# A depthwise convolution's running sums in a PSUM tile of two banks, and two banks instead of four for small products

## The chip, the cores and the metric

The kernel runs on one core of a Trainium2 chip. The core has five engines with instruction streams of their own: TensorE (PE; its weight loads are listed as PEld), VectorE (DVE), ScalarE (ACT), GpSimd (POOL) and SyncE (SP), which issues nearly all DMAs here. The metric is the device time of one execution in microseconds; lower is better.

## What is computed

The reference is one inference step of a decoder with two layers, for a prompt of 512 tokens (with 16 leading tokens before it) and eight samples of 8 tokens. The change touches layer 0. There one input projection feeds two branches: A, a gated unit, a causal depthwise convolution of width 31, a LayerNorm over channels, a swish and a projection; and B, a complex state space (S5) with its own projections. Each branch is gated, and an output projection follows:

```python
def _conformer_conv(u, g, buf, conv_w, conv_b, ln_g, ln_b, pw):
    h = u * jax.nn.sigmoid(g)
    hp = jnp.concatenate([buf.astype(h.dtype), h], axis=1)
    y = lax.conv_general_dilated(hp, conv_w.astype(h.dtype)[:, None, :], window_strides=(1,), padding='VALID',
                                 dimension_numbers=('NWC', 'WIO', 'NWC'), feature_group_count=W_A)
    y = y + conv_b.astype(h.dtype)
    y = jax.nn.silu(_ln(y, ln_g, ln_b)).astype(u.dtype)
    y = y @ pw.astype(u.dtype)
    return y, hp[:, -(CONV_W - 1):]

def _even_layer(x, conv_buf, s_re, s_im, ev, j):
    proj = x @ ev['w_in'][j].astype(x.dtype)
    u_a, g_a, z_a, u_b, z_b = _split(proj, EVEN_SIZES)
    y_a, new_buf = _conformer_conv(u_a, g_a, conv_buf, ...)
    y_b, new_re, new_im = _s5(u_b, s_re, s_im, ...)
    mix = jnp.concatenate([y_a * jax.nn.silu(z_a), y_b * jax.nn.silu(z_b)], axis=-1).astype(x.dtype)
    out = mix @ ev['w_out'][j].astype(x.dtype)
    ...
```

Layer 1 (an mLSTM branch and an RWKV branch) is not touched.

## The kernel before, in words

All 592 token columns (528 of the prompt with its leading tokens, 64 of the samples) stay on chip with channels on the 128 partitions. A projection goes by stripes of 128 output columns: for each of the 16 blocks of inputs, the weights are split into a high part `wh` (a cast on ACT) and a low part `wl` (a subtraction on DVE, from `wraw` and `wh`), the operands likewise into `xh` and `xl`, and PE adds three products for each of two spans of 296 columns into two PSUM banks of the tag `acc`. The weights come in pieces of four blocks, with two buffers each of `wh` and `wl`; one piece feeds 24 products.

Layer 0's first part runs as a set of threads in `layer0` (line 843). `Weave.run` (line 323) chooses at build time the order of each engine's instructions, by an estimated timeline with costs per instruction (`cost`, line 239) and a priority for each thread; on the chip every engine takes its stream in that order. A thread can ask for a PSUM bank by its tag and wait for it. Beside the four `acc` banks, four banks have the tag `sps`, for small products: the S5 tables (`s5_inject_tables`, `s5_tables`), the S5 injections and outputs (`s5_inject`, `s5_out`), the LayerNorm's sums (`ColNorm`) and, at the start, the third stripe of the first bundle of projections. ACT copies the small products out (`s5m`, `s5xv`, `s5kt`, `s5y`).

The threads around the change: `convs` (line 1033) calls `conv_taps` (line 831) for each of eight channel blocks. The input `hh` of a block is made on DVE from a projection's PSUM banks and a gate (`glu`, line 912). The block's result `cc` is made by 31 taps, each of two DVE instructions, one over the 528 prompt columns and one over the 64 sample columns: the first tap a tensor_scalar, the other 30 a scalar_tensor_tensor that multiplies a shifted view of `hh` by the tap's weight (a column of `par`) and adds `cc`, into `cc`. `norms` then subtracts the shift from `cc` on POOL, squares it on ACT and adds both to the sums on POOL. `s5_chain` is a recurrence over 66 chunks for each half of the states, with three small POOL products a step (tiles `s5c` and `s5xv`). After the norms and S5's outputs, `norms` makes the operands `cbh` and `cbl` of the next projection. The gate stripes of the input projection (`gates`) are spread between the convolution's blocks by the number of finished blocks, `S.taps`; those that are left follow.

All instructions that go through the threads are recorded under one line, L321, so that the tiles' names tell them apart.

Of the kernel before, what the change touches and what calls it, by code (L numbers as in the profile page):

```python
# [11 lines left out]
F32 = mybir.dt.float32  # L12
F32R = mybir.dt.float32r
# [7 lines left out]
NT = 592  # L21
K1, K2 = 354, 532            # columns of parameters and constants of RWKV, where layer 0 has two of S5's tables
NP = 528
SPAN0 = ((0, 296), (296, 592))
SPAN1 = ((16, 304), (304, 592))
SPANR = ((14, 302), (302, 592))            # the leading tokens have no outputs; the last one shifts into the prompt
SPAN2 = ((16, 336), (336, 592))
NZ = 5           # gate stripes with the RWKV phase
MIX1 = [8, 9, 10, 11, 12, 13, 0, 1, 2, 3, 4, 5, 14, 15, 6, 7]     # as they become ready
# [7 lines left out]
# ------------------------------------------------------------------ host side  # L37

def _consts():
    """Shape-only constants, packed: of both layers, of RWKV, of mLSTM."""  # L40
# [16 lines left out]
    # mLSTM: invalid entries carry 200  # L57
# [10 lines left out]
    c["rreset"] = np.broadcast_to(reset, (128, 128))       # of a chunk, of the samples  # L68
    c["own"] = (p[:, None] // 16 == np.arange(64)[None, :] // 8) & (p[:, None] % 8 == np.arange(64)[None, :] % 8)
    # rows of a sample token: K = high, low, high part; V = high, high, low part  # L70
# [19 lines left out]
def _gp(v):  # L90
    """[64 groups, 64 states, ...] -> [(g2, p), g', ...]"""
    v = v.reshape((32, 2, 64) + v.shape[2:])
    v = np.moveaxis(v, 0, 2)
    return v.reshape((128, 32) + v.shape[3:])
# [14 lines left out]
def layout(x):  # L109
# [48 lines left out]
        x["state_mlstm_c"][0].reshape(8, 4, 2, 128, 256).transpose(1, 0, 3, 2, 4))   # h b kp kb v  # L158
    a["rs0"] = np.ascontiguousarray(
        x["state_rwkv_s"][0].transpose(1, 3, 0, 2).reshape(8, 128, 8, 64))            # pair (h k) b v  # L160
# [6 lines left out]
    a["w_m"] = _stripes(np.concatenate([w[:, 0:4096], w[:, 4104:5128]], 1))           # q k v o zc  # L167
# [3 lines left out]
    a["w_r"] = _stripes(w[:, 5128:9352])                                              # r k v wa zd  # L171
# [16 lines left out]
def unlayout(r):  # L188
# [3 lines left out]
    conv = r["o_conv"].transpose(1, 2, 0)                                     # 9 30 1024  # L192
# [10 lines left out]
# ---------------------------------------------------------------- device side  # L203
# [5 lines left out]
class Engine:  # L209
    """An engine whose instructions are emitted later: each call gives one to yield."""  # L210
# [11 lines left out]
def delay(p, e):  # L222
    """us from a result of engine p to its use by engine e."""
    if p == e:
        return {"G": 0.1, "D": 2.0}.get(e, 0.0)
    if e == "T":
        return {"A": 0.3, "V": 0.23, "G": 0.2}.get(p, 1.2) + MT
    return {"T": 0.2, "G": 0.08, "D": 1.2}.get(p, 0.14) + (MV if e == "V" else MA)


def part(z):
    """What of a tile an operand is."""
    return z.name, z.offset, tuple(z.ap)


SAME = {"V": 0.13, "A": 0.14}              # us from a result to its use by the same engine


def cost(e, fn, out, ins):
    """Estimate in us."""  # L240
# [6 lines left out]
    cols = sum(z.shape[1:] == (1,) for z in ins) * (n > 1)         # per-partition scalars  # L247
# [15 lines left out]
class Weave:  # L263
    """Emits threads of instructions, with each engine's in the order of an estimated timeline.  A thread yields
    instructions, conditions to wait for, or the tag of a PSUM bank to get.  Low priority numbers go first."""
# [13 lines left out]
    def ready(self, op):  # L279
        """When an instruction's operands are there."""  # L280
# [3 lines left out]
        for z in ins + [out]:  # L284
            f, p = self.done.get(z.name, (0.0, e))
            if z is not out or e != "D" or p != "D":          # loads of parts of a tile don't wait for each other
                t = max(t, f + delay(p, e))
            if p == e and e in SAME:
                t = max(t, self.at.get(part(z), 0.0) + SAME[e])
# [33 lines left out]
    def run(self, threads):  # L323
        """threads: (priority, generator)."""
# [44 lines left out]
def both(*gens):  # L369
    """Emits generators by turns; their values."""  # L370
# [11 lines left out]
def run(gen):  # L382
    """Emits a generator straight; its value."""
# [7 lines left out]
def straight(K, gen):  # L391
    """Emits a thread without a Weave; its value."""
# [48 lines left out]
def resident(K, pool, W, s):  # L441
    """Stripe s of W, split, all of it on chip."""
# [11 lines left out]
def dense_s(K, ws, rhs, span, out=None):  # L454
    """Products of several resident stripes over one span, by turns."""
# [11 lines left out]
def weights(K, W, s, k0):  # L467
    """Blocks k0 .. k0 + 4 of W's stripe s as exact parts."""
# [11 lines left out]
def dense_g(K, W, s, nk, rhs, spans, acc=None, early=()):  # L480
    """acc[i] = (W stripe s)^T x over spans[i]; operands as exact pairs H + L; the first weights may be there."""
# [19 lines left out]
def banks(K, **n):  # L501
    """The four PSUM banks beside those of dense(), by tag."""
# [5 lines left out]
class ColNorm:  # L508
    """LayerNorm over channels, blocks of 128 on partitions: sums about the mean of the first block."""
# [13 lines left out]
    def shift(self, x):  # L523
        """From the first block."""
# [5 lines left out]
    def add(self, j, x, pool, sl=slice(None), e=None):  # L530
        """Block j, less the shift."""
# [11 lines left out]
    def finish(self, i):  # L543
        """mean (less the shift) and 1/std of span i, on every partition."""
# [15 lines left out]
def exp_ops(V, x, n, r, e):  # L560
    """x <- exp(x), accurate to float32 rounding; instructions, with three temporaries (the last of integers)."""
# [12 lines left out]
# ---- S5  # L574

def s5_setup(K, pool, S):
# [54 lines left out]
    # q = (a - 1) / lambda  # L631
# [36 lines left out]
def s5_state(K, pool, S, hf):  # L668
    """State columns of half hf (16 group pairs): 0 = X_0 (prompt), 1..66 = injections, then X_1..X_66,
    67..74 injections of the samples, 75..82 their initial states."""  # L670
# [14 lines left out]
def s5_inject_tables(K, pool, S, j):  # L685
    """Injections of stripe j (8 groups) into chunk states, by place in the chunk."""
# [20 lines left out]
def s5_inject(K, pool, S, j, m3, u):  # L707
    """Chunk injections of stripe j into S.xv."""
# [36 lines left out]
def s5_tables(K, pool, S, j):  # L745
    """Output tables of stripe j: C a^d (re, -im) and the causal in-chunk kernel."""
# [40 lines left out]
def s5_out(K, pool, S, j, tables, u, yb, ahead):  # L787
    """Outputs of stripe j; a load goes ahead of the last steps."""
# [27 lines left out]
    # gelu (tanh form)  # L816
# [12 lines left out]
# ---- layer 0  # L829

def conv_taps(K, P, j, h, c):
    """Depthwise convolution of h [30 old | prompt | 8 x (30 old, 8 new)]."""
    cw = P["convw"][:, 31 * j:31 * j + 31]
    hs, cs = (z.rearrange("p (b t) -> p b t", b=8) for z in (h[:, 558:], c[:, NP:NT]))
    for k in range(31):
        for o, src in ((c[:, 0:NP], h[:, k:k + NP]), (cs, hs[:, :, k:k + 8])):
            if k == 0:
                yield K.V.tensor_scalar(o, src, cw[:, 0:1], P["convb"][:, j:j + 1], op0=OP.mult, op1=OP.add)
            else:
                yield K.V.scalar_tensor_tensor(o, src, cw[:, k:k + 1], o, op0=OP.mult, op1=OP.add)  # L840


def layer0(K, O):
# [3 lines left out]
    with mk("l0") as p0:  # L847
# [3 lines left out]
        with banks(K, sps=4), mk("ln0") as pl, mk("cc", 8) as pc, mk("zs") as pz, ExitStack() as mid, \  # L851
                tc.manual_schedule(engines=MANUAL):
            cv, p5 = (mid.enter_context(mk(n)) for n in ("cv", "s5"))
            w = Weave(K, dict(sps=4, acc=4))
# [20 lines left out]
            def pair(x, e=None):  # L875
                """x as exact parts in place of an operand that is no longer needed."""
# [10 lines left out]
            # results of the input projection  # L887

            def inputs(j, tag):
# [8 lines left out]
                # the first three stripes' weights, between the blocks of X  # L898
# [41 lines left out]
            # results of the branches' last projections  # L940
# [54 lines left out]
            # S5: tables one item ahead of their use  # L995
# [37 lines left out]
            def convs():  # L1033
                for j in range(8):
                    yield lambda: len(H) > j
                    c = pc.tile([128, NT], F32, name="cc")
                    yield from conv_taps(K, P, j, H[j], c)
# [32 lines left out]
            def loads_z():  # L1070
                """The gates, again."""
# [35 lines left out]
def out_proj(K, W, M, res, P, spans, y=None, bias=None, early=(), nxt=None):  # L1107
    """x' = LayerNorm(ALPHA x + mix W).  To the rows of y; or as operands with a copy in DRAM (less the bias), and the
    products of two stripes of the next layer."""
# [4 lines left out]
    with K.tc.tile_pool(name="op", bufs=1, reuse_waits="tile") as po:  # L1114
# [9 lines left out]
        for j in range(16):  # L1124
# [15 lines left out]
            if j < 13:  # L1140
                if j < len(early):
                    # two stripes by turns, while the operands become ready
# [10 lines left out]
        # the last stripes by span, so that one span's normalisation runs beside the other's products  # L1153
# [49 lines left out]
# ---- RWKV-7 (pairs of heads on 128 partitions; token columns: 16 leading + 48 zero, 8 chunks of 64, 8 x 8 samples)  # L1203
# [8 lines left out]
class Job:  # L1212
    """A stripe's products, and what comes after.  paired: of a stripe of at most 64 columns, whose weights' two parts
    are columns of one operand.  final: the operands' blocks are free after it.  Without spans: only its
    first weights.  X: operands of its own.  tag: of its PSUM banks."""
# [7 lines left out]
def dense_threads(K, w, jobs, X):  # L1223
    """Threads of the jobs (a generator of jobs, tuples of jobs that take turns, or conditions) with operands X:
    loads, splits, products, results."""
# [79 lines left out]
def shift_mix(K, w, pool, P, i, acc, sh, out, spans, tag="acc"):  # L1305
    """Token shift of stripe i of the shifted projections, in a bank "acc" and one tag; its last tokens go to sh."""
# [20 lines left out]
def rwkv_setup(K, w, pool, P, R):  # L1327
    """Operands with the two heads as diagonal blocks keep their zeros all along."""
# [13 lines left out]
def exact_sum(K, w, pool, R, m, x):  # L1342
    """m^T x in a bank, of a matrix m that float32r holds."""
# [13 lines left out]
def rwkv_front(K, w, pool, P, R, j, g):  # L1357
    """Five chunks of head pair j, columns 320 g .. 320 g + 320: decays, rates, directions, keys."""
# [32 lines left out]
    yield tt(V, kk, kk, q, OP.mult)                          # normalised key direction  # L1391
# [8 lines left out]
    yield A.activation(sg, sg, AF.Exp, scale=-ED)            # decay up to the previous token  # L1400
# [11 lines left out]
    yield V.scalar_tensor_tensor(a, a, 1.0, k, op0=OP.add, op1=OP.mult)      # the key used  # L1412
# [8 lines left out]
def rwkv_back(K, w, pool, P, R, j, g):  # L1421
    """Their products, and the inverses of their triangles' blocks."""
# [17 lines left out]
    # products of keys with directions and receptances, masked; [(h s), (A t | R t)]  # L1440
# [878 lines left out]
```

## Time and profile before

| | us |
|---|---|
| median of 3 runs | 2829.81 (2828.62 to 2831.03) |
| profiled execution, first to last instruction | 2825.2 |
| PE busy | 2633.6 (93%) |
| DVE busy | 1709.9 (61%) |
| ACT busy | 1065.1 (38%) |
| POOL busy | 1043.5 (37%) |

The times of the runs are those of the whole execution; the span of the profile goes from its first to its last instruction. Busy shares are averages over stages with different limits, so the slices and the stretches of time are to be read before them. "Released by" in a row names the engine and the tile whose instruction ended a wait.

### The profile page before, as it was taken

The numbers are of one execution on the slowest core, as the hardware profiler recorded it, in microseconds if no ns is written. First come the engines' busy times: TensorE is split into PE (matmuls) and PEld (weight loads), VectorE is DVE, ScalarE is ACT, GpSimd is POOL, SyncE is SP. The second block draws the span as 40 slices with busy tenths as digits, with TensorE's granted clock in tenths as the row PEclk, the third lists the DMA queues.
The fourth block names the chain that finished last, engine by engine and source line by source line (L and its number), as shares of the span: only waits on it lengthen the run. The fifth ranks groups of instructions, "written<-read, shape, count | busy, mean of one in ns | idle before, by whom it ended". The sixth has DMA issues, their size and how long they took to land. (4 is left out here: it accounts for less than half of the span.)

```text
span 2825.2 us, 49626 instructions
## 1 busy us (share of the span) xinstructions
PE 2633.6 (93%) x18848; PEld 2543.2 (90%) x18848; DVE 1709.9 (61%) x3282; ACT 1065.1 (38%) x2291; POOL 1043.5 (37%) x1776
## 2 busy tenths in 40 slices
PE   8977888689999999999999999999999999999996
PEld 8977788689999999998998999889999889898996
DVE  7667986687343436666667667677664444446337
ACT  4312221135222223455455355455433333344223
POOL 1886688850000222335235234434300212112443
PEclk9998998899999999999999999999999999999998
DMA  6322332235433333321222222222333424335333
GB/s 195 91 79 72 98 83 83 65 103 146 127 105 108 105 105 102 117 85 62 65 77 67 79 80 72 69 72 69 93 109 95 127 84 131 114 105 164 120 111 106
DMA packets 202095, 278.33 MB, mean 99 GB/s; under 512 B 66808, under 2 KB 86008, under 8 KB 201856
## 3 DMA queue, kind: packets, MB, share of 16 engines
q1 hardware_dynamic: 199552, 270.30, 31.9%
q10 hardware_dynamic: 2304, 4.85, 0.4%
q8 instruction: 148, 2.42, 0.4%
q14 instruction: 91, 0.75, 0.1%
HBM read 232.54 MB, written 42.53 MB: 97 GB/s over the span
## 5 line engine op out<-in xcount | busy, mean ns | idle before, releaser
L321 PE MATMUL acc<-xh,wh 128*128 128x296 f32 (+1 forms) x3520 | 813.1, 308 | 46.9 <-ACT wh L321 38.2
L321 PE MATMUL acc<-xh,wl 128*128 128x296 f32 (+2 forms) x3488 | 805.2, 308 | 45.9 <-DVE wl L321 45.8
L321 PE MATMUL acc<-xl,wh 128*128 128x296 f32 (+1 forms) x3520 | 810.6, 307 | 0.0
L321 PEld LDWEIGHTS acc<-xh,wh 128*128 128x128 f32 x3520 | 587.8, 193 | 55.4 <-ACT wh L321 40.0
L321 DVE TENSOR_TENSOR wl<-wraw,wh 128x512 fp32r<-128x512 f32 x492 | 383.3, 779 | 414.7 <-ACT wh L321 389.0
L321 PEld LDWEIGHTS acc<-xh,wl 128*128 128x128 f32 x3488 | 580.2, 193 | 58.7 <-DVE wl L321 51.5
L321 PEld LDWEIGHTS acc<-xl,wh 128*128 128x128 f32 x3520 | 586.7, 192 | 5.6 <-issue 2.3
L321 ACT CAST wh<-wraw 128x512 fp32r<-128x512 f32 (+1 forms) x496 | 305.7, 618 | 731.8 <-PE acc L321 642.2
L321 DVE SCALAR_TENSOR_TENSOR cc<-hh,par,cc 128x528 f32<-128x528 f32 x480 | 266.0, 615 | 0.0
L490 PE MATMUL acc<-xh,wh 128*128 128x296 f32 (+2 forms) x832 | 182.1, 299 | 0.0
L490 PE MATMUL acc<-xh,wl 128*128 128x296 f32 (+1 forms) x832 | 180.7, 298 | 0.8 <-DVE wl L434 0.8
L490 PE MATMUL acc<-xl,wh 128*128 128x296 f32 (+2 forms) x832 | 180.6, 297 | 0.0
L433 ACT CAST wh<-wraw 128x512 fp32r<-128x512 f32 x100 | 62.1, 621 | 209.4 <-PE acc L490 206.8
L490 PEld LDWEIGHTS acc<-xh,wl 128*128 128x128 f32 x832 | 131.5, 188 | 1.4 <-DVE wl L434 1.3
L490 PEld LDWEIGHTS acc<-xh,wh 128*128 128x128 f32 x832 | 132.0, 189 | 0.5 <-ACT wh L433 0.2
L490 PEld LDWEIGHTS acc<-xl,wh 128*128 128x128 f32 x832 | 132.0, 188 | 0.4
L434 DVE TENSOR_TENSOR wl<-wraw,wh 128x512 fp32r<-128x512 f32 x100 | 68.8, 689 | 96.7 <-ACT wh L433 91.0
L1151 POOL TENSOR_TENSOR rr<-rr,lna 128x592 f32<-128x592 f32 (+1 forms) x2 | 3.5, 1744 | 309.0 <-ACT lna L404 309.0
L321 POOL TENSOR_TENSOR rnt<-rcf,rn 128x75 f32<-128x75 f32 (+14 forms) x240 | 85.1, 355 | 81.1 <-DMA rcf<-rcd 64.7
L404 POOL TENSOR_TENSOR lnb<-lnb,rr 128x592 f32<-128x592 f32 (+1 forms) x24 | 42.1, 1755 | 186.3 <-DVE rr L1120 186.3
L321 POOL TENSOR_TENSOR k<-mc,mch 128x512 fp32r<-128x512 f32 x32 | 42.4, 1324 | 155.5 <-ACT mch L321 136.0
L321 ACT ACT_TABLE_LOAD x71 | 91.1, 1283 | 16.2 <-DVE rh L321 14.4
(576 smaller groups left out, 4880.7 us busy)
## 6 DMA issues: line engine op xcount, KB each, us to landing
wraw<-w_e SPq DMA_DIRECT2D x160, 256.0 KB, 3.3
wraw<-w_m SPq DMA_DIRECT2D x160, 256.0 KB, 3.0
wraw<-w_r SPq DMA_DIRECT2D x132, 256.0 KB, 3.1
wraw<-w_eo SPq DMA_DIRECT2D x64, 256.0 KB, 3.0
wraw<-w_oo SPq DMA_DIRECT2D x64, 256.0 KB, 3.0
rcf<-rcd SPq DMA_DIRECT2D x16, 640.0 KB
wraw<-w_glu SPq DMA_DIRECT2D x32, 256.0 KB, 2.9
mc<-mc SPq DMA_DIRECT2D x32, 256.0 KB, 3.1
```

Source lines behind the costliest of these rows:

```text
L321: getattr(eng.e, fn)(out, *a, **kw)
L404: getattr(eng.e, fn)(out, *a, **kw)
L433: K.nc.scalar.copy(H, x)
L434: (e or K.nc.vector).tensor_tensor(L, x, H.bitcast(F32), op=OP.subtract)
L490: K.nc.tensor.matmul(o, w[:, kk], x[:, a:b], start=st, stop=sp)
L1151: G.tensor_tensor(r, r, N.c, op=OP.subtract)
```

## The change

Each block's running sums stand in one PSUM tile `taps` of 128 x 1024 floats, that is two banks, from the first tap to the last but one; the last tap reads it and writes the block's result to `cc` in SBUF. The pool of small products `sps` has two banks instead of four, in the pool and in the planner. Number, order and shapes of the taps are the same, and the planner's cost of a tap too. The rest of the diff takes comments and docstrings away.

```diff
-def conv_taps(K, P, j, h, c):
+def conv_taps(K, P, j, h, c, acc):
     cw = P["convw"][:, 31 * j:31 * j + 31]
-    hs, cs = (z.rearrange("p (b t) -> p b t", b=8) for z in (h[:, 558:], c[:, NP:NT]))
+    b8 = lambda z: z.rearrange("p (b t) -> p b t", b=8)
+    hs = b8(h[:, 558:])
     for k in range(31):
-        for o, src in ((c[:, 0:NP], h[:, k:k + NP]), (cs, hs[:, :, k:k + 8])):
+        for sl, cut, src in ((slice(0, NP), lambda z: z, h[:, k:k + NP]), (slice(NP, NT), b8, hs[:, :, k:k + 8])):
+            o = cut((c if k == 30 else acc)[:, sl])
             if k == 0:
                 yield K.V.tensor_scalar(o, src, cw[:, 0:1], P["convb"][:, j:j + 1], op0=OP.mult, op1=OP.add)
             else:
-                yield K.V.scalar_tensor_tensor(o, src, cw[:, k:k + 1], o, op0=OP.mult, op1=OP.add)
+                yield K.V.scalar_tensor_tensor(o, src, cw[:, k:k + 1], cut(acc[:, sl]), op0=OP.mult, op1=OP.add)
...
-        with banks(K, sps=4), mk("ln0") as pl, mk("cc", 8) as pc, mk("zs") as pz, ExitStack() as mid, \
+        with banks(K, sps=2), mk("ln0") as pl, mk("cc", 8) as pc, mk("zs") as pz, ExitStack() as mid, \
...
-            w = Weave(K, dict(sps=4, acc=4))
+            w = Weave(K, dict(sps=2, acc=4))
+            taps = K.ss.tile([128, 1024], F32, name="taps", bufs=1)
...
-                    yield from conv_taps(K, P, j, H[j], c)
+                    yield from conv_taps(K, P, j, H[j], c, taps)
```

## Rows read from the trace of the kernel before

**Rows 1.** The page's slices, 40 of 70.6 us: busy tenths, granted TensorE clock.

```profile
PE   8977888689999999999999999999999999999996
PEclk9998998899999999999999999999999999999998
```

**Rows 2.** Stretches: us, then busy us (instructions) of PE, PEld, DVE, ACT, POOL; clock.

```profile
70.00:630.00 560.00, 458.27 (x3215) 450.47 (x3215) 422.51 (x690) 134.20 (x252) 428.77 (x672) 0.91 0.32 85
...
700.00:770.00 70.00, 70.00 (x515) 70.00 (x514) 25.50 (x42) 20.29 (x34) 0.00 (x0) 1.00 0.44 131
```

**Rows 3.** Waits of PE, 70 to 630 us: total us, times, longest us.

```profile
PE acc L321 <- DVE wl L321: 45.8, 21, 6.5
PE acc L321 <- ACT wh L321: 38.2, 6, 13.7
PE sps L321 <- POOL s5xpad L321: 17.8, 1, 17.8
```

**Rows 4.** Timeline of ACT and PE near 218 us: start, us, work, idle before.

```profile
216.91 0.70 ACT L321 ACTIVATE st<-cc 128x592 f32<-128x592 f32 x1 [18.58 <-POOL cc L321]
...
218.17 0.61 PE L321 MATMUL acc<-xh,wh 128*128 128x296 f32 x1 [13.67 <-ACT wh L321]
```

**Rows 5.** POOL's groups by form, 70 to 630 us: busy us, mean ns, idle before.

```profile
L321 POOL TENSOR_TENSOR s5c<-s5a,s5xv 128x64 f32<-128x64 f32 x132 | 73.6, 558 | 9.2
L321 POOL TENSOR_TENSOR s5xv<-s5xv,s5c 128x32 f32<-128x32 f32 x132 | 63.9, 484 | 9.5
L321 POOL TENSOR_TENSOR s5c<-s5c 128x32 f32<-128x32 f32 x132 | 61.5, 466 | 9.3
```

**Rows 6.** The same groups, 200 to 215 us.

```profile
L321 POOL TENSOR_TENSOR s5c<-s5a,s5xv 128x64 f32<-128x64 f32 x14 | 4.9, 349 | 1.1
L321 POOL TENSOR_TENSOR s5xv<-s5xv,s5c 128x32 f32<-128x32 f32 x14 | 3.8, 269 | 1.1
L321 POOL TENSOR_TENSOR s5c<-s5c 128x32 f32<-128x32 f32 x14 | 3.5, 252 | 1.1
```

**Rows 7.** DVE's costliest groups by form, 70 to 630 us.

```profile
L321 DVE SCALAR_TENSOR_TENSOR cc<-hh,par,cc 128x528 f32<-128x528 f32 x240 | 198.2, 826 | 0.0
L321 DVE TENSOR_TENSOR wl<-wraw,wh 128x512 fp32r<-128x512 f32 x110 | 103.4, 941 | 95.7 <-ACT wh L321 90.9 <-DMA s5ul<-ub 4.6
L321 DVE SCALAR_TENSOR_TENSOR cc<-hh,par,cc 128x64 f32<-128x64 f32 x240 | 97.0, 404 | 0.0
```

**Rows 8.** The same groups, 598 to 605 us.

```profile
L321 DVE SCALAR_TENSOR_TENSOR cc<-hh,par,cc 128x528 f32<-128x528 f32 x7 | 5.3, 760 | 0.0
L321 DVE SCALAR_TENSOR_TENSOR cc<-hh,par,cc 128x64 f32<-128x64 f32 x7 | 1.9, 277 | 0.0
L321 DVE TENSOR_TENSOR wl<-wraw,wh 128x512 fp32r<-128x512 f32 x2 | 1.4, 683 | 0.0
```

**Rows 9.** Timeline of DVE and of POOL, 141.7 to 143.3 us (neighbours are merged).

```profile
141.49 1.06 DVE L321 SCALAR_TENSOR_TENSOR cc<-hh,par,cc 128x64 f32<-128x64 f32 x2
142.47 0.89 DVE L321 TENSOR_TENSOR hh<-sg,acc 128x296 f32<-128x296 f32 x3
...
141.86 0.80 POOL L321 TENSOR_TENSOR s5c<-s5c 128x32 f32<-128x32 f32 x1
142.74 0.28 POOL L321 TENSOR_TENSOR s5xv<-s5xv,s5c 128x32 f32<-128x32 f32 x1
```

**Rows 10.** DVE's groups by form, 70 to 630 us: one tensor_scalar of S5's output.

```profile
L321 DVE TENSOR_SCALAR s5y<-s5y 128x592 f32<-128x592 f32 x7 | 9.9, 1415 | 0.1
```

**Rows 11.** Timeline of PE at 737 us: the first product of the next projection.

```profile
737.05 0.44 PE L321 MATMUL acc<-cbh,wh 128*128 128x296 f32 x2
```

**Rows 12.** DVE's groups by form, 0 to 800 us: one with a PSUM tensor and a scalar column.

```profile
L321 DVE SCALAR_TENSOR_TENSOR sz<-acc,par,sz 128x296 f32<-128x296 f32 x2 | 1.0, 522 | 2.0 <-PE acc L321 2.0
```

**Rows 13.** ACT's groups by form, 70 to 630 us: the weight cast and one copy.

```profile
L321 ACT CAST wh<-wraw 128x512 fp32r<-128x512 f32 x110 | 67.7, 619 | 242.1 <-PE acc L321 214.5 <-DVE wl L321 8.5 <-DVE cc L321 8.0
...
L321 ACT COPY s5m<-sps 128x512 f32<-128x512 f32 x14 | 8.2, 588 | 9.4 <-PE sps L321 9.2
```

## The prediction, made before the changed kernel was built or run

> **What bounds the kernel now.** The first view to read is the page's line of slices [rows 1]. From slice 10 on TensorE (PE) is busy in nearly every slice at a granted clock of 9 tenths or more; in slices 2 to 9, roughly 70 to 640 us, its digits are 6 to 9 and so are the clock's. Time can come back only there. The stretches put figures on it [rows 2]. From 700 to 770 us PE never stops: 515 instructions in 70 us, 0.1359 us each, clock 1.00 (the 2.4 GHz level). From 70 to 630 us it is busy 458.3 of 560 us with 3215 instructions at a mean clock of 0.91, which is pieces at 2.4 GHz and pieces at 1.2 GHz. At the full pace they would take 3215 x 0.1359 = 437 us. So 123 us are lost: 101.7 us idle, and 458.3 - 437 = 21 us in slower products; the clock is below 1.00 only in this stretch with the idle spells.
>
> The waits say who ends PE's idle time [rows 3]: 45.8 us for `wl` (DVE), 38.2 us for `wh` (ACT), 17.8 us for `s5xpad` (POOL), together the whole 101.7. One must not stop at the engine that is named. In the timeline around 218 us [rows 4] PE has waited 13.7 us for ACT's `wh`; ACT itself had waited 18.6 us for POOL's `cc`; and POOL had not been idle, it was late, as follows. In the 70 to 630 us stretch POOL works through two recurrences of 66 steps, three small products each, which take 558, 484 and 466 ns on average [rows 5]; with DVE idle, between 200 and 215 us, the same three take 349, 269 and 252 ns [rows 6]. That is 132 x (1508 - 870) ns = 84 us of lateness on POOL. DVE shows the mirror image: the taps of 528 and 64 columns take 826 and 404 ns on average and the `wl` split 941 [rows 7], against 760, 277 and 683 where POOL is idle [rows 8].
>
> Two neighbours in one timeline show what does it [rows 9]. Beside a tap, whose two tensors both lie in SBUF, POOL's product takes 0.80 us (252 ns alone). Right after it DVE runs the three `hh<-sg,acc` products, one tensor in SBUF and one in PSUM, three in 0.89 us, and POOL's product beside them takes 0.28 us (269 ns alone). So DVE and POOL hold each other up when DVE reads two SBUF tensors, and don't when one of the two is in PSUM. The taps are the largest such work: 198.2 + 97.0 us of DVE.
>
> **The change part by part.**
>
> *The sums move to PSUM.* Of 496 tap instructions 480 are scalar_tensor_tensor. All lose their second SBUF tensor: `hh` stays in SBUF, the sum is read from PSUM. No instruction is added; the last tap of each stripe writes `cc` where it stood before, so POOL's and ACT's norm work follows as now. The next stripe's first tap must follow the last tap of this one, on the same engine and in that order already: no wait is added, and nothing is moved past a queue.
>
> What DVE gets back: 240 x (826 - 760) + 240 x (404 - 277) ns = 16 + 30 = 46 us of its excess; of the rest, `wl` has 110 x (941 - 683) ns = 28 us, the S5 output's work some 25 us (its tensor_scalar alone averages 1415 ns [rows 10]). Those keep meeting POOL. The taps are then half of the excess, so I take half of PE's waits for `wl` as gone: 23 of 45.8 us.
>
> What POOL gets back: of DVE's work that meets POOL, the taps (295 us) are about three quarters, `wl` (103 us) most of the rest. Three quarters of 84 us is 63 us; the 21 us left, ten per recurrence, are less than the single waits of 13.7 and 17.8 us in which the lateness ended, each after 30 or more us of it. So of the waits for `wh` and `s5xpad`, 38.2 + 17.8 = 56 us, I let 5 stand: 51 back.
>
> The slow products: they came with the idle spells, so they go in proportion. 74 of 101.8 us idle is 0.73; 0.73 x 21 = 15 us.
>
> Sum: 23 + 51 + 15 = 89 us. Nothing further on eats it: the products of the input projection alone keep PE busy until 737 us [rows 11], 100 us after the norms and S5 are through on POOL and DVE, so no later step is next in line when these end earlier, and behind 737 us PE is the bound to the last few slices [rows 1].
>
> *The price of a tap in PSUM.* Reading: the nearest row is a scalar_tensor_tensor with per-partition scalar and one PSUM tensor, 522 ns for 296 columns [rows 12]. The clean taps [rows 8] give (760 - 277)/464 = 1.04 ns a column and a fixed 211 ns; 522 - 308 leaves 214. So reading costs nothing. Writing PSUM from DVE is in no row. Below: it can't gain, since PE's pace is the floor anyway. Above: reading and writing one bank could halve the rate, 0.55 + 0.07 us per pair. I take nothing, by the nearest row. The cover: DVE's clean load in the stretch is 240 x 1.04 + 110 x 0.68 + about 45 for the rest = 370 us of the 437 that PE needs, so some 70 us can hide, if spread; as the taps come in runs, I count on half, 35 us or 0.07 us per tap.
>
> The Trainium skill has a rule against this change: "Perfetto Trace Analysis", Optimizing Scalar/DVE Operations, puts DVE's access overhead at about 60 ns on SBUF and 125 ns on PSUM. By it 480 x 65 ns = 31 us would be added to DVE, and the time would be 31 us above my sum were none of it hidden. For the read the rows disagree, 214 against 211 ns.
>
> *The first tap* (16 instructions, tensor_scalar) writes PSUM too; at a clean tap's pace [rows 8] all of them take 8 x 1.04 = 8 us, and even if that were all new it would lie in the slack above. Nothing either way.
>
> *Two banks instead of four.* The first bundle of projections holds two such banks while it runs, before the taps. Later S5's table thread and its output thread hold at most one each, and the norm one, at the end two. Each of the 54 small products (16 pairs of `s5xv` copies, 14 `s5m`, 16 `s5y`, 8 `s5kt`) can now wait for the copy two before it instead of four. From below: nothing, as the order is planned with the bank count. From above: each waits for a whole copy, 0.59 us at most, and a `wh` cast of 0.62 us ahead of it on ACT [rows 13]: 54 x 1.21 = 65 us. As ACT is busy 134 of 560 us [rows 2], I take nothing and keep 65 for the range.
>
> **The rivals.** *Banks become the wait*: PE stands in front of small products for ACT's copies. For: PE takes everything in order, so one late copy stops the projections as well. Against: ACT's load. Two thirds of the upper price, 43 us of the 89: 2784.
>
> *Slower taps*, the rival on the other side: reading and writing the same bank at half rate costs 240 x 0.62 = 148 us on DVE; 35 hidden leaves 113, less the gain of 89: 2854. It decides from (89 + 35)/480 = 0.26 us per tap. For: no row shows DVE writing PSUM. Against: reading PSUM is as fast as SBUF.
>
> *The change doesn't do what it says*: POOL is held up as before, because `par`'s scalar column still comes from SBUF beside `hh` and no row shows that with a PSUM tensor while POOL works. Then 2830, up to 2840. Against: S5's tensor_scalar without any tensor but its own meets POOL too [rows 10], so something other than the scalar column makes a DVE instruction collide. The Trainium skill ("SBUF — State Buffer", Who interferes with whom) explains such one-tensor cases by fast modes that take both read ports; by it the taps in PSUM would be free.
>
> **How the numbers follow.** The profiled span is 2825.2 us, the median of the three runs 2829.8, 4.6 us more; 2829.8 - 89 = 2741 us, a span near 2736. Chances: forecast 0.75 (2708 to 2775; 2708 is the median less nearly all the 123 us), banks 0.10 (2784), slower taps 0.07 (2854), no release 0.06 (2830 to 2840), 0.02 for the rest. The range takes in the forecast and the banks: 2708 to 2795. About 0.2%, 6 us, is what a measurement of this kernel can tell from no change. Faster 0.86, within 0.05, slower 0.09.
>
> **What would show it.** The recurrence's products at 350, 270 and 250 ns also beside taps; taps near 760 and 277 ns everywhere; PE busy near 437 us for as many instructions, idle 20 to 30 us, mostly for `wl`; the clock near 1.00 in the stretch; the first `cbh` product near 650 us. Waits of PE in front of `sps` products would speak for the banks; taps above 1.0 us for the third rival; recurrence products at 480 ns for the last. I'd be wrong in size if the plan's order leaves PE holes of its own that the lateness now covers.

## The result, and the profile after

| | before | after |
|---|---|---|
| median of 4 runs each, us | 2830.42 (2828.62 to 2836.24) | 2767.04 (2762.25 to 2772.02) |
| ratio, 95% interval | | 0.9777 (0.9764 to 0.9791) |
| profiled span, us | 2825.2 | 2760.5 |

The change makes the kernel 63 us faster; the forecast was 89 us faster, 2741 us. The measured time lies in the range, 26 us from the forecast value. These 26 us are what the rest is about.

The page's slices of the kernel after [rows 1]: of slices 2 to 9 three are still at 8, the others at 9; the clock is at 9 in all but the last slice of the kernel.

```profile
PE   8998899899999998999999999999999999999996
PEclk9999999999999999999999999999999999999998
```

The stretch 70 to 630 us of after (us, then busy us and instructions of PE, PEld, DVE, ACT, POOL; clock) [rows 2]:

```profile
70.00:630.00 560.00, 515.41 (x3696) 503.79 (x3695) 455.59 (x763) 169.41 (x305) 354.42 (x673) 0.98 0.39 101
```

PE gets through 3696 instructions instead of 3215. At the pace of the undisturbed stretch these need 3696 x 0.1359 = 502 us, so 58 us are lost where 123 were: 45 us idle and 13 us of slower products. 123 - 58 = 65 us is the whole difference of the two spans (64.7). It is got back before 670 us; the first product of the next projection, from PE's timeline of after [rows 11], comes 66.5 us sooner:

```profile
670.54 0.44 PE L321 MATMUL acc<-cbh,wh 128*128 128x296 f32 x2
```

PE's waits of after, 70 to 630 us [rows 3]. The waits for ACT's `wh` and for `s5xpad`, in which POOL's lateness ended, are nearly gone: 2.8 of 56 us are left, 6.3 us with three small waits that are new; 5 were forecast. Those for `wl` are 38.2 us, where 23 were forecast:

```profile
PE acc L321 <- DVE wl L321: 38.2, 34, 5.1
PE acc L321 <- ACT wh L321: 2.8, 1, 2.8
PE sps L321 <- DVE cc L321: 1.5, 1, 1.5
PE sps L321 <- POOL lnb L321: 1.0, 1, 1.0
PE sps L321 <- DMA s5m<-kz: 1.0, 1, 1.0
```

POOL's recurrence products of after, by form [rows 5, 6]: 1053 ns for the three, against 1508 before and 870 where DVE was idle. The 24 us left (132 x 183 ns) answer the 21 forecast:

```profile
L321 POOL TENSOR_TENSOR s5c<-s5a,s5xv 128x64 f32<-128x64 f32 x132 | 51.0, 386 | 9.2
L321 POOL TENSOR_TENSOR s5xv<-s5xv,s5c 128x32 f32<-128x32 f32 x132 | 45.2, 342 | 9.5
L321 POOL TENSOR_TENSOR s5c<-s5c 128x32 f32<-128x32 f32 x132 | 42.9, 325 | 9.3
```

DVE's groups of after, by form [rows 7, 8]. The taps' durations are those of undisturbed ones before (760 and 277 ns), as forecast. But in the last column the taps, which had no idle time before them, now have some:

```profile
L321 DVE SCALAR_TENSOR_TENSOR taps<-hh,par,taps 128x528 f32<-128x528 f32 x232 | 179.1, 772 | 7.4
L321 DVE TENSOR_TENSOR wl<-wraw,wh 128x512 fp32r<-128x512 f32 x130 | 109.3, 841 | 65.2 <-ACT wh L321 60.7 <-DMA s5ul<-ub 4.4
L321 DVE SCALAR_TENSOR_TENSOR taps<-hh,par,taps 128x64 f32<-128x64 f32 x232 | 66.6, 287 | 5.7
L321 DVE TENSOR_TENSOR s5q<-s5q,s5y 128x592 f32<-128x592 f32 x8 | 23.0, 2875 | 0.1
```

The timelines show what that small idle time stands for. In DVE's (start, us, work; neighbours of one kind are merged under the first one's name) a row x5 that begins with a narrow tap is narrow, wide, narrow, wide, narrow. Before, such a row took 2.03 us, POOL being idle:

```profile
333.33 2.03 DVE L321 SCALAR_TENSOR_TENSOR cc<-hh,par,cc 128x64 f32<-128x64 f32 x5
```

After, it takes 2.55 us, whether POOL works or not:

```profile
175.91 2.55 DVE L321 SCALAR_TENSOR_TENSOR taps<-hh,par,taps 128x64 f32<-128x64 f32 x5
```

Start to start, a wide tap before a narrow one took 0.680 us and takes 0.808; a narrow before a wide one took 0.197 and takes 0.325 (medians over the stretch). Before, a tap starts some 0.08 us *before* the recorded end of the last one; after, 0.035 us behind it. That is 0.128 us a step. It is not paid at `wl` behind a wide tap (0.680 still), nor by the narrow last tap behind the wide last tap, whose results go to `cc` (0.680).

What it does to PE is a regular pattern. DVE's timeline of after, three pieces of weights, six taps between two `wl`:

```profile
167.57 0.68 DVE L321 TENSOR_TENSOR wl<-wraw,wh 128x512 fp32r<-128x512 f32 x1
168.18 3.36 DVE L321 SCALAR_TENSOR_TENSOR taps<-hh,par,taps 128x64 f32<-128x64 f32 x6
171.44 0.68 DVE L321 TENSOR_TENSOR wl<-wraw,wh 128x512 fp32r<-128x512 f32 x1
172.04 3.36 DVE L321 SCALAR_TENSOR_TENSOR taps<-hh,par,taps 128x64 f32<-128x64 f32 x6
175.31 0.68 DVE L321 TENSOR_TENSOR wl<-wraw,wh 128x512 fp32r<-128x512 f32 x1
```

and PE's beside it, the rows with a wait:

```profile
168.31 0.54 PE L321 MATMUL acc<-xh,wl 128*128 128x296 f32 x2 [0.34 <-DVE wl L321]
172.18 0.54 PE L321 MATMUL acc<-xh,wl 128*128 128x296 f32 x2 [0.33 <-DVE wl L321]
176.04 0.54 PE L321 MATMUL acc<-xh,wl 128*128 128x296 f32 x2 [0.33 <-DVE wl L321]
```

DVE needs 171.44 - 167.57 = 3.87 us for a `wl` and six taps; PE needs 24 x 0.1359 = 3.26 us for the 24 products of a piece. So PE loses 0.61 us a piece: 0.33 us shows as a wait, the rest is in the products at its edges (the pair behind it takes 0.54 us, the others 0.43 or 0.44), while the granted clock is 1.00 from 168 to 176 us. With the steps of before DVE would need 0.61 + 3 x 0.877 = 3.24 us, just under PE's 3.26. Of the 132 stretches between two `wl` from 70 to 640 us, 33 hold six taps: an estimated 33 x 0.61 = 20 us, of which 33 x 0.28 = 9 us count above as slower products, though not for a lower clock.

### The profile page after: what moved, and what is told of

It reads as the page before. It is cut to its first block, busy times and chain, and to the rows that moved or that the text cites. A ratio compares the mean times of both kernels' runs of the same rounds, so it can differ in the third digit from the quotient of the medians.

```text
span 2760.5 us, 49648 instructions
## 1 busy us (share of the span) xinstructions
PE 2624.8 (95%) x18848; PEld 2530.0 (92%) x18848; DVE 1692.7 (61%) x3282; ACT 1065.4 (39%) x2291; POOL 963.7 (35%) x1776
## 5 line engine op out<-in xcount | busy, mean ns | idle before, releaser
L321 PE MATMUL acc<-xh,wl 128*128 128x296 f32 (+2 forms) x3488 | 801.4, 306 | 38.2 <-DVE wl L321 38.2
L321 DVE TENSOR_TENSOR wl<-wraw,wh 128x512 fp32r<-128x512 f32 x492 | 375.5, 763 | 381.3 <-ACT wh L321 359.1
L321 DVE SCALAR_TENSOR_TENSOR taps<-hh,par,taps 128x528 f32<-128x528 f32 x464 | 245.7, 530 | 13.0
L434 DVE TENSOR_TENSOR wl<-wraw,wh 128x512 fp32r<-128x512 f32 x100 | 70.0, 701 | 95.9 <-ACT wh L433 90.3
```

Source lines behind the costliest of these rows:

```text
L321: getattr(eng.e, fn)(out, *a, **kw)
L434: (e or K.nc.vector).tensor_tensor(L, x, H.bitcast(F32), op=OP.subtract)
```

## The experiments

The program has something to go with the new step. An instruction that needs another's result waits for a count of instructions done on that one's engine. Before, in a run of taps, a tap waits for the instruction two back on DVE, its own column range's last tap. After, it waits for the one just before it, a tap of other columns. The theory: this wait costs the 0.128 us. Rivals: PSUM itself is slow from a write to the next access; or the other long DVE instructions beside POOL (`s5q`, above: 2875 ns) make the waits for `wl`.

**The banks alone.** The kernel before with:

```diff
-        with banks(K, sps=4), ...
+        with banks(K, sps=2), ...
-            w = Weave(K, dict(sps=4, acc=4))
+            w = Weave(K, dict(sps=2, acc=4))
```

> The running sums stay in SBUF as before; only the pool of small products has two banks instead of four. Theory (banks cost and give nothing): 2830 us, within 6 us of the kernel before; POOL's three recurrence products at about 1500 ns together (558, 484, 466 before), first cbh product near 737 us, PE's waits in front of sps products under 3 us in 70 to 630 us apart from the one for s5xpad. Rival (the planner's order, which it makes with the bank count, is where part of the 63 us comes from): 2767 to 2815 us. Rival (two banks make PE wait, and the tap's move gained more than 63 us): 2840 us or more.

Measured: 2830.2 us, ratio to before 1.0014 (1.0004 to 1.0024), so 1 to 7 us slower. Its PE waits, 70 to 630 us, are those of before [rows 3]:

```profile
PE acc L321 <- DVE wl L321: 45.4, 15, 6.5
PE acc L321 <- ACT wh L321: 35.0, 4, 13.3
PE sps L321 <- POOL s5xpad L321: 17.8, 1, 17.8
```

The recurrence products take 1507 ns. So two banks give nothing and take at most a few us, and the gain is all the taps'.

**Which side of the tap frees POOL, and which makes the step.** Two kernels, each the kernel after with one side put back to SBUF. First the writes (the read stays in PSUM):

```diff
-            o = cut((c if k == 30 else acc)[:, sl])
+            o = cut((c if k else acc)[:, sl])
```

> The kernel after with one edit: from the second tap on the taps write the SBUF tile and read as their sum what the first tap left in PSUM; so the accumulation over taps is left out, the number, shapes and order of the instructions stand. Theory (the second SBUF tensor that is read is what holds POOL up): as free as the kernel after, recurrence products near 1050 ns together, taps near 770 and 287 ns. The step from tap to tap on DVE (start to start) back at 0.68 and 0.20 us, against 0.81 and 0.33 after, since no tap writes the tile that the next one reads; then 2735 to 2750 us. Rival (the SBUF write counts as well): products between 1200 and 1500 ns, 2790 to 2830 us. Rival for the step (a tap that reads PSUM starts late by itself): 0.81 and 0.33 stay, about 2767 us.

Measured: 2750.6 us (one execution), just above the 2750 us expected at most. Steps 0.675 and 0.192 us; taps 753 and 270 ns. POOL by form, 409 + 337 + 315 = 1061 ns:

```profile
L321 POOL TENSOR_TENSOR s5c<-s5a,s5xv 128x64 f32<-128x64 f32 x132 | 54.0, 409 | 9.2
L321 POOL TENSOR_TENSOR s5c<-s5c 128x32 f32<-128x32 f32 x132 | 44.5, 337 | 9.3
L321 POOL TENSOR_TENSOR s5xv<-s5xv,s5c 128x32 f32<-128x32 f32 x132 | 41.5, 315 | 9.5
```

PE's waits for `wl`:

```profile
PE acc L321 <- DVE wl L321: 23.4, 11, 5.2
```

Then the reads (the write stays in PSUM):

```diff
-            o = cut((c if k == 30 else acc)[:, sl])
+            o = cut((c if k in (0, 30) else acc)[:, sl])
...
-                yield K.V.scalar_tensor_tensor(o, src, cw[:, k:k + 1], cut(acc[:, sl]), op0=OP.mult, op1=OP.add)
+                yield K.V.scalar_tensor_tensor(o, src, cw[:, k:k + 1], cut((acc if k == 30 else c)[:, sl]), op0=OP.mult, op1=OP.add)
```

> The mirror image: the first tap writes SBUF, taps 2 to 30 read as their sum what the first one left in SBUF (beside hh, two SBUF tensors) and write the PSUM tile; the last reads that. The accumulation over taps is left out. Theory (two SBUF tensors that are read hold POOL up, where the result goes doesn't matter): recurrence products back near 1500 ns, taps beside POOL near 0.83 and 0.40 us, 2825 to 2850 us. Rival (the write port is the shared thing): products near 1050 ns, about 2767 us. For the step from tap to tap: no tap reads what the one before wrote, so 0.68 and 0.20 us where POOL is idle; 0.81 and 0.33 would say that writing PSUM is late by itself.

Measured: 2834.7 us (one execution). POOL by form:

```profile
L321 POOL TENSOR_TENSOR s5c<-s5a,s5xv 128x64 f32<-128x64 f32 x132 | 68.8, 521 | 9.2
L321 POOL TENSOR_TENSOR s5xv<-s5xv,s5c 128x32 f32<-128x32 f32 x132 | 56.1, 425 | 9.5
L321 POOL TENSOR_TENSOR s5c<-s5c 128x32 f32<-128x32 f32 x132 | 54.7, 414 | 9.3
```

1360 ns, the taps 880 and 412 ns: DVE and POOL hold each other up again. So the second SBUF tensor that is *read* does it, and the result's place doesn't matter. The products are 140 ns under the 1500 expected; probably POOL gets through in the pauses, for the steps here are 0.813 and 0.329 us. Those were not expected: no tap reads what the last one wrote. They leave two readings, writing PSUM or the wait, for in this program too each tap waits for the one just before it.

**One tile or two.** First the columns cut at the bank's end, in one tile of two banks as in the kernel after: 512 columns in the first, 80 in the second (the last 16 prompt columns as two blocks of 8 beside the samples' eight; ACT makes the two blocks' inputs with two small copies).

```diff
-        for sl, cut, src in ((slice(0, NP), lambda z: z, h[:, k:k + NP]), (slice(NP, NT), b8, hs[:, :, k:k + 8])):
+        for sl, cut, src in ((slice(0, 512), lambda z: z, h[:, k:k + 512]), (slice(512, NT), b10, hs[:, :, k:k + 8])):
...
+                    yield A.copy(h[:, 558:596], h[:, 512:550])
+                    yield A.copy(h[:, 596:634], h[:, 520:558])
```

> The kernel after, computing the same, with the tile's columns cut at the bank's end: each tap is one instruction of 512 prompt columns (all in the first bank) and one of 80 columns (ten blocks of 8, the last 16 prompt columns as two blocks beside the eight samples; all in the second bank). In the kernel after the 528 prompt columns reach 16 columns into the bank of the sample columns, and in the program each tap waits for the tap instruction just before it, where before it waited for the one two back. Theory (that wait is the price of 0.125 us per tap): start to start about 0.67 and 0.22 us, 0.88 to 0.90 us per pair instead of 1.13; PE's regular gaps of 0.33 us in runs of taps are gone, waits for wl near 28 us instead of 38, and 2740 to 2755 us. Rival (PSUM's own delay between a tap's write and the next one's read): about 1.13 us per pair stays and 2767 us, within 6. Rival (the steps shorten but the waits for wl come from the collisions of s5q with POOL alone): 0.88 us per pair and 2760 to 2767 us.

Measured: 2765.5 us, ratio 0.9788 (0.9769 to 0.9806); steps 0.792 and 0.341 us. A row x5 of its timeline:

```profile
169.06 2.56 DVE L321 SCALAR_TENSOR_TENSOR taps<-hh,par,taps 128x80 f32<-128x80 f32 x5
```

No gain; but the cut had not changed the program's wait either. Though the two parts share no column and no bank, each tap still waits for the one before it. So the same kernel with two tiles of one bank each, in which it waits for the one two back:

```diff
-            taps = K.ss.tile([128, 1024], F32, name="taps", bufs=1)
+            taps = [K.ss.tile([128, 512], F32, name="taps%d" % i, bufs=1) for i in range(2)]
...
```

> As in split, 512 prompt columns and 80 others, but the two parts of the sum stand in two PSUM tiles of one bank each instead of one tile of two banks; all is computed. In the program of split each tap still waits for the tap instruction just before it, here for the one two back, as in the kernel before. Theory (the wait on the instruction just before is the price): start to start about 0.66 and 0.21 us, 0.88 us per pair, PE's waits for wl near 23 us as in read_only, 2744 to 2757 us. Rival (the delay is PSUM's: a tap that writes it holds up the next instruction that touches it, whichever bank): 0.79 and 0.34 us as in split, 2760 to 2770 us.

Measured: 2741.9 us (2736.9 to 2747.7), ratio 0.9703 (0.968 to 0.9725); steps 0.658 and 0.208 us. A row x5:

```profile
161.56 2.03 DVE L321 SCALAR_TENSOR_TENSOR taps<-hh,par,taps 128x80 f32<-128x80 f32 x5
```

A `wl` and six taps, with no wait of PE beside them:

```profile
166.49 0.68 DVE L321 TENSOR_TENSOR wl<-wraw,wh 128x512 fp32r<-128x512 f32 x1
167.09 2.69 DVE L321 SCALAR_TENSOR_TENSOR taps<-hh,par,taps 128x80 f32<-128x80 f32 x6
169.70 0.68 DVE L321 TENSOR_TENSOR wl<-wraw,wh 128x512 fp32r<-128x512 f32 x1
```

169.70 - 166.49 = 3.21 us. The stretch 70 to 630 us and PE's waits in it:

```profile
70.00:630.00 560.00, 532.51 (x3864) 526.34 (x3863) 439.25 (x777) 179.00 (x333) 356.04 (x672) 0.98 0.40 106
```

```profile
PE acc L321 <- DVE wl L321: 13.4, 6, 5.5
PE acc L321 <- ACT wh L321: 10.6, 3, 4.5
PE sps L321 <- POOL s5xpad L321: 1.4, 1, 1.4
```

Same operations, same columns, same two banks, all computed; only the wait differs, and with it 24 us. So the wait is the price, and PSUM's own delay is ruled out: a pair of taps takes 0.866 us in PSUM, 0.877 in SBUF. This version is faster than both kernels.

**The same wait in SBUF.** The kernel before, with the prompt tap one column wider, so that the two parts overlap:

```diff
-        for o, src in ((c[:, 0:NP], h[:, k:k + NP]), (cs, hs[:, :, k:k + 8])):
+        for o, src in ((c[:, 0:NP + 1], h[:, k:k + NP + 1]), (cs, hs[:, :, k:k + 8])):
```

> The kernel before, sums in SBUF, with the prompt tap one column wider (529 instead of 528), so that it also adds into the first sample column; that column's sums are no longer the reference's, the work is the same but for 1 column. As the two instructions of a tap now overlap in one column, each waits for the one just before it. Theory (the wait itself costs the 0.13 us, wherever the sum stands): start to start 0.81 and 0.33 us where POOL is idle, against 0.680 and 0.197 before. Rival (waiting so costs this only when the sum is in PSUM): 0.68 and 0.20 us. The time by either: 2825 to 2845 us, since POOL is held up here as before and its lateness covers part of DVE's, as in write_only.

Measured: 2834.2 us (one execution; before on the same chip 2826.9); steps 0.808 and 0.320 us where POOL is idle.

```profile
179.78 2.54 DVE L321 SCALAR_TENSOR_TENSOR cc<-hh,par,cc 128x64 f32<-128x64 f32 x5
```

The wait costs the same with all in SBUF. Here it adds 7 us in the one execution; as POOL is late here too, PE's waits change their names more than their sum: `wl` 64.5 instead of 45.8 us, but `wh` 19.8 instead of 38.2 and `s5xpad` 9.1 instead of 17.8 [rows 3]. The recurrence products, 527 + 418 + 406 = 1351 ns, are again shorter than before (1508), as they were with the same steps in the kernel with the read put back.

**The long `s5q` products.** In the kernel after, one of them at 255.78 us took 4.68 us beside POOL's table products, and PE's longest wait, 5.1 us, followed. They go to POOL:

```diff
-    yield V.tensor_tensor(q, q, y, op=OP.mult)
+    yield G.tensor_tensor(q, q, y, op=OP.mult)
```

> The kernel after with one edit: the eight products s5q times s5y of S5's output (two SBUF tensors, 592 columns, 2.9 us each beside POOL's table products, 0.77 us by itself) go to POOL. Theory (a DVE instruction that starves beside POOL holds up the wl behind it and costs some 12 us of PE's 38 us of waits for wl, and a like share of the slow products): waits for wl 24 to 30 us, no single one above 3 us, 2750 to 2759 us. Rival (POOL's eight added products of about 1.5 us, 12 us, and the handovers to POOL and ACT come back as waits for wh and s5xpad): 2762 to 2772 us.

Measured: 2763.1 us, ratio 0.9773 (0.9754 to 0.9792), no different from the kernel after.

```profile
PE acc L321 <- DVE wl L321: 33.5, 34, 3.8
PE acc L321 <- ACT wh L321: 3.6, 3, 1.7
```

The longest wait shrinks to 3.8 us, but there are as many, `wl` itself takes 880 instead of 841 ns (131 x 39 ns = 5 us back), and the next product of S5's output that reads two SBUF tensors, `s5y<-s5q,s5y`, 1916 instead of 931 ns (8 us back). The theory of 12 us fell. Both edits together, two tiles and `s5q` on POOL:

> two_tiles and s5q_pool together. Theory (two separate causes): the two gains add up, 2733 to 2746 us, waits for wl 10 to 15 us, the largest part of what is left being wl itself beside POOL (841 against 683 ns). Rival (the same waits counted twice, since DVE's lateness from either cause is made up between runs of taps): no better than the better of the two by 4 us.

Measured: 2737.9 us, ratio 0.9692 (0.9671 to 0.9712), not told apart from two tiles alone; waits for `wl` 15.7 us. The time lies in the theory's range, but so does that of two tiles alone. The gains don't add; `s5q` had none to add.

**An order that knows of the wait.** The kernel after, with one term in the planner:

```diff
-                t = max(t, self.at.get(part(z), 0.0) + SAME[e])
+                t = max(t, self.at.get(part(z), 0.0) + SAME[e], f + 0.05 if z.name.startswith("taps") else 0.0)
```

> The kernel after with one edit in the planner: it lets an instruction that touches the tile taps begin no sooner than 0.05 us after the last one that did, as the chip does; so it may put other DVE work between two taps. Theory (the runs of taps have nothing else ready to stand between them, since the next wl waits for its weights' buffer, which PE frees at its own pace): of the about 360 pairs of taps that are neighbours on DVE nearly all stay, 2760 to 2770 us. Rival (the order can hide the wait): a third of them or more broken up, 2745 to 2757 us.

Measured: 2754.3 us, ratio 0.9747 (0.9731 to 0.9763), some 9 to 13 us better than after. The theory was right that the taps stay neighbours (374 of 480 stand right behind a tap, 384 after), and wrong that nothing can be hidden. The planner puts fewer taps between two `wl`: six in 22 stretches (33 after), four in 20 (5 after).

```profile
167.07 0.68 DVE L321 TENSOR_TENSOR wl<-wraw,wh 128x512 fp32r<-128x512 f32 x1
167.68 2.22 DVE L321 SCALAR_TENSOR_TENSOR taps<-hh,par,taps 128x64 f32<-128x64 f32 x4
169.81 0.68 DVE L321 TENSOR_TENSOR wl<-wraw,wh 128x512 fp32r<-128x512 f32 x1
```

PE's waits for `wl` are 12 instead of 34:

```profile
PE acc L321 <- DVE wl L321: 28.1, 12, 5.0
PE acc L321 <- ACT wh L321: 7.8, 3, 3.8
```

How much of it is the `s5q` products, which now take 1320 ns, can't be told from this run.

**The narrow part in SBUF.** As with two tiles, but the 80 columns stay in `cc`, and the small products have three banks:

```diff
-            taps = [K.ss.tile([128, 512], F32, name="taps%d" % i, bufs=1) for i in range(2)]
+            taps = K.ss.tile([128, 512], F32, name="taps", bufs=1)
...
+            o = cut((c if k == 30 or sl.start else acc)[:, sl])
...
+                yield K.V.scalar_tensor_tensor(o, src, cw[:, k:k + 1], cut((c if sl.start else acc)[:, sl]), op0=OP.mult, op1=OP.add)
...
```

> 512 prompt columns of the sums in one PSUM bank, the 80 others (ten blocks of 8) in SBUF as before; the pool of small products has three banks; all is computed. Each tap waits for the instruction two back. Theory (only the wide taps matter to POOL, the narrow ones are a sixth of the columns, and banks are worth 0 to 4 us): narrow taps 0.29 us alone and up to 0.42 beside POOL, recurrence products 1100 to 1200 ns together against 1067 in two_tiles, 2742 to 2757 us. Rival (POOL's short products are held up by any instruction with two SBUF tensors, however narrow): 1250 ns or more, 2765 us or more. Rival (the third bank is worth more than the narrow taps cost): below 2738 us.

Measured: 2763.1 us (2751.9 to 2763.3), ratio 0.9766 (0.9745 to 0.9787): 18 to 21 us above two tiles, more than the theory had. POOL loses little (1097 ns), as it said; DVE is held up instead:

```profile
L321 DVE SCALAR_TENSOR_TENSOR cc<-hh,par,cc 128x80 f32<-128x80 f32 x240 | 98.4, 410 | 0.0
```

410 against 294 ns in PSUM, 240 x 116 ns = 28 us of DVE, and the waits for `wl` are 25.9 instead of 13.4 us. That is the likely cause of the 18 to 21 us; as the third bank and with it the planner's order differ too, it isn't shown apart.

## Why the prediction was right, and where it was short

- *Two SBUF reads hold DVE and POOL up; the taps in PSUM don't.* Right, shown by the pair of kernels with one side put back. The rule of the Trainium skill, "SBUF — State Buffer", Who interferes with whom, that a DVE instruction with two SBUF inputs contends with a GpSimd instruction reading SBUF, agrees: 1061 ns with the write in SBUF, 1360 with the read there.
- *POOL's return, 51 us.* Right: 2.8 us are left of 56, 6.3 with the new small waits (5 forecast).
- *The waits for `wl`, 23 us back, and the slow products, 15 us.* Short: 38.2 us are left where 23 were to be, and 13 us of slower products where 21 - 15 = 6 were to be. 15 + 7 = 22 of the 26 us; the others come to 1 us more than forecast, and some 2 are the difference between the profiled executions, whose spans are 24 us from the forecast (2760.5 against 2736), and the medians. The slower products didn't go in proportion to the idle time because short waits cost PE at their edges as well, an estimated 9 of the 13 us.
- *The price of a tap in PSUM.* This is the step that failed, in three ways. It said that no wait is added, looking only at the first tap of a stripe; but the wait of each tap that stands right behind another had moved from the instruction two back to the one just before. Two tiles against one, with that wait the only difference, is worth 24 us of the 26. It priced the tap by durations, 214 against 211 ns, and these stayed right: the price is between the instructions, where no duration shows it (0.128 us from start to start). And it covered a price with 70 us of free DVE time in the stretch, half of it counted. But in the runs of taps, where it is paid, a `wl` and six taps take 3.24 of PE's 3.26 us even at the old steps: nearly no cover. (The 70 us were too few, if anything: the 370 us of load add durations that overlap, 1.04 us for a clean pair of taps that takes 0.877 from start to start.)
- *The size, from there.* With the wait gone the lost time is 560 - 3864 x 0.1359 = 35 us, where 123 - 89 = 34 were forecast, and the time is 2742 us (0.9703 x 2829.8 = 2746 by the ratio) where 2741 were. That it meets so closely is luck: of the 27.5 us idle, 13.4 are waits for `wl` where 23 were to be left, and 14.1 other waits where 5 were. That the kernel after lies in the range is owed to the range's width: the forecast's part alone reaches from 2708 to 2775 us, and the term put at nothing fits into it.
- *The Trainium skill's rule against the change* ("Perfetto Trace Analysis", Optimizing Scalar/DVE Operations: about 60 ns on SBUF, 125 on PSUM; 31 us by estimate). It would have given 2772 us with nothing hidden, near the 2767 measured, but not for its reason: two tiles read and write PSUM as much, and the pair of taps takes 0.866 us against 0.877 in SBUF.
- *Banks*: right within a few us (1 to 7). *Slower taps*: the mechanism named, one bank read and written at half rate, isn't there; a smaller price stood in its place, 0.128 us against the 0.26 from which it would have decided. *No release of POOL*: ruled out.
- *Two readings of rows 1 were off.* The clock's digits in slices 2 to 9 are 8 and 9, not 6 to 9, and the last slice has an 8 too, so the clock isn't below 1.00 in this stretch alone. No term of the sum rests on it.

## What to carry to other kernels

When a tile moves, look in the program at what each instruction waits for, not only at how long it takes: a wait on the instruction just before on the same engine costs a step that no duration shows (here 0.12 to 0.13 us), so read start to start. Two independent sums that alternate in PSUM should stand in tiles of their own, lest the one be taken to depend on the other; in SBUF the two ranges of one tile `cc` were told apart. And count cover in the block in which the price is paid (here DVE's work per piece of weights against PE's), not over the stretch.

## What the hardware showed beside

- A DVE instruction that waits for the one just before it starts 0.12 to 0.13 us later than one that waits for the one two back: 0.808 against 0.680 and 0.320 against 0.197 us in SBUF, 0.792 against 0.658 and 0.341 against 0.208 in PSUM. The Trainium skill, "VectorE: DVE Perf Modes", The DRAIN you can't avoid, has that a semaphore after each of eight copies costs nothing extra against one after the last. For these taps a wait on the instruction just before does cost, and the measurement decides.
- The scalar column that the taps read from SBUF beside `hh` doesn't make them meet POOL: in the kernel after the wide ones take 772 ns on average beside POOL's work and 772 without it (760 without it before).
- A DVE product of two SBUF tensors beside POOL's back-to-back table products took up to 4.68 us for 592 columns (2875 ns on average after, 1777 before). Taking it away brought no time that could be measured.
